# Frames ahead of weights at the start, the low-rank block alternating with its neighbour, and the recurrence's first loads on GpSimd's queue

## The chip, the cores and the metric

The kernel runs on one core of a Trainium2 chip. The metric is the device time of one execution in microseconds (us). Engines are named as in the profile: PE (TensorE matmul), PEld (its weight loads), DVE (VectorE), ACT (ScalarE), POOL (GpSimd), SP (SyncE, which here only issues DMAs). Each engine works through its own list of instructions in order, and waits at the head of that list for what the instruction there needs.

## The reference

One layer on 2048 frames of 1024 features, all in float32. A combined projection feeds a diagonal state space model (S5), a delta-rule recurrence (RWKV-7) and two gates; the branches are merged, projected, and followed by a feed-forward block with squared ReLU.

```
h = rmsnorm(x, norm1_g)
proj = h @ w_in                       # 1024 -> 512 + 1792 + 2048
u, p_rwkv, gate_a, gate_b = split(proj)
o_a = s5_branch(u)                    # 32 groups of 16 channels, scan over time, gelu, half-GLU
o_b = rwkv7_branch(p_rwkv)            # token shift, low-rank decay, state update per frame
merged = sigmoid(gate_a) * (o_a @ wb_a) + sigmoid(gate_b) * (o_b @ wb_b)
x = x + merged @ w_out
x = x + relu(rmsnorm(x) @ w1)**2 @ w2
out = rmsnorm(x)
# in rwkv7_branch: pm = p + (prev_frame(p) - p) * mu, cut into r, k, v, xg, xw, xa
# decay from tanh(xw) @ w2, a = sigmoid(a0 + xa @ a2), g = sigmoid(xg) @ g2
```

## The kernel before

Every large product is done as three matmuls on split operands: a weight w is cast to a rounded part (`wh`, on ACT or DVE) and a rest (`wl = w - wh`, on POOL), the same for the activations (`hh`, `hl`), and `mm3` (lines 121 to 123) issues wh x hl, wl x hh, wh x hh into the same PSUM tile. A window is 512 frames; there are NW = 4 of them. A block is one m (128 output features) of one window, 8 x 3 = 24 matmuls.

The program has four phases; the change is in the first two.

Phase A. `norm_window` loads four tiles of 128 frames (`xt`, line 452), sums their squares on ACT (line 145), makes the scale `rsa`, `rqa` on POOL (147, 149), scales on DVE (455), transposes on PE (462) and evicts into `hh` and `hl` (465, 466). `wu_load` loads the four blocks of the u projection (`wur`, 490), casts on DVE (491) and subtracts on POOL in two halves (493). At the start the two generators are woven step by step. Then come the u blocks, and then `dense()`: the projection for the recurrence, blocks m = 17, 16, 4 to 15, each for all four windows before the next. A block's PSUM tile (tag `mm`, four of them, shared with the low-rank products) is evicted by ACT (547) and DVE (548, 551, 555: the shift by one frame), into an `sg` tile (three of them), and stored to DRAM (`pm_d`). Block p17_w feeds `low_rank(w)`: a tanh, a split into `xh`, `xl`, and four pieces of six matmuls (`lr`, line 580) with two sigmoids each (`lo`, 583); a list `side` holds these pieces, and two are taken from it in each following block. `dense()` is woven with `s5_stream`, the S5 branch, eight groups q of channels: projections on PE (`px`, line 268), a scan on DVE (lines 380 to 403), products on PE and a gelu on ACT.

Phase B. `load(s)` reads the recurrence's inputs of 128 frames from DRAM (rm, km, vm, sgx, sig, aa). `elem(s)` prepares them (`kr`, then `sq`, `xh`, `xl`, the norm `n`, the scan `e`, `kf`, `km`, `BK`, `AG` and so on), `inv(s)` inverts small triangular systems, `chain(s)` runs the recurrence itself (`R` line 893, `U`, `S`, `y` line 915). They go in turns with `gates()`, the projection of the gates: `loadw` brings a weight block (`gwr`, then `gwh`, `gwl` 959) and 16 tiles of h (`gh`, 969) for a window; 64 blocks `gp` fill PE beside the recurrence.

Phases C and D (merge, output projection, feed-forward) follow and are not touched.

The order on each engine is not the program's order everywhere: a scheduler may move an instruction ahead of others on its engine where its operands allow it, unless `keep_in_program_order` (in the code: `pin`) holds it. In phase A and B the order of the generators' steps decides what stands where.

Of the kernel before, what the change touches and what calls it, by code (L numbers as in the profile page):

```python
# [21 lines left out]
NK = DM // 128  # L22
# [404 lines left out]
def phase_a(tc, nc, K, io, u_d, pm_d, h_d, z_d):  # L427
    with ExitStack() as st:
# [13 lines left out]
        with ExitStack() as s2:  # L442
# [68 lines left out]
        def load(m):  # L511
            wr = wp.tile([128, NK, 128], F32, tag="wr", name=f"wr{m}", bufs=1)
            nc.sync.dma_start(wr, io["win"][m])
            wh = wp.tile([128, NK, 128], F32R, tag="wh", name=f"wh{m}")
            wl = wp.tile([128, NK, 128], F32R, tag="wl", name=f"wl{m}")
            nc.scalar.copy(wh, wr)
            nc.gpsimd.tensor_tensor(wl, wr, wh, op=ALU.subtract)
            return wh, wl

        def dense():  # L520
            late = Late()
            nxt = first
            side = []
            for mi, m in enumerate(order):
                wh, wl = nxt
                if mi + 1 < len(order):
                    nxt = load(order[mi + 1])
                last = None
                if m % 3 == 0 and m < 16:
                    w = m // 3 - 2  # L530
                    o = 512 * (w % 2)
                    for j, H in enumerate((HH, HL)):
                        tc.keep_in_program_order(
                            nc.sync.dma_start(h_d[j, w], H[w // 2][:, :, o:o + 512].bitcast(F32)))
                i = m - 4
                for w in range(NW):
                    pp = psm.tile([128, 512], F32, tag="mm", name=f"p{m}_{w}")
                    o = 512 * (w % 2)
                    for k in range(NK):
                        mm3(nc, pp, wh[:, k], wl[:, k], HH[w // 2][:, k, o:o + 512], HL[w // 2][:, k, o:o + 512],  # L540
                            k == 0, k == NK - 1)
                        if k == 3:
                            yield
                        if side and k in (2, 6):
                            side.pop(0)()
                    sg = wp.tile([128, 512], F32, tag="sg", name=f"sg{m}_{w}", bufs=3)
                    nc.scalar.activation(sg, pp, ACTF.Copy, scale=om[:, i:i + 1])
                    nc.vector.scalar_tensor_tensor(sg[:, 1:512], pp[:, 0:511], mu[:, i:i + 1], sg[:, 1:512],
                                                   op0=ALU.mult, op1=ALU.add)
                    if w:  # L550
                        nc.vector.scalar_tensor_tensor(sg[:, 0:1], last, mu[:, i:i + 1], sg[:, 0:1],
                                                       op0=ALU.mult, op1=ALU.add)
                    if w < NW - 1:
                        last = wp.tile([128, 1], F32, tag="lc", name=f"lc{m}_{w}")
                        nc.vector.tensor_copy(last, pp[:, 511:512])
                    if m == 17:
                        side.extend(low_rank(w, sg))
                    else:
                        if m == 16:
                            nc.scalar.activation(sg, sg, ACTF.Sigmoid)  # L560
                        late.put(lambda i=i, w=w, sg=sg: nc.sync.dma_start(
                            pm_d[128 * i:128 * i + 128, 512 * w:512 * w + 512], sg))
                    yield
            late.flush()
# [35 lines left out]
def phase_b(tc, nc, K, io, pm_d, ob_d, h_d, gt_d, inv_d):  # L600
    V, A, P, T = nc.vector, nc.scalar, nc.gpsimd, nc.tensor
    NS = S // 128
    with ExitStack() as st:
# [46 lines left out]
        def load(s):  # L650
            d = D[s]
            for i, n in enumerate(("rm", "km", "vm")):
                d[n] = xp.tile([128, 4, 128], F32, tag=n, name=f"{n}{s}", bufs=3 if n == "vm" else 2)
                nc.sync.dma_start(d[n], pm_d[512 * i:512 * i + 512, 128 * s:128 * s + 128].rearrange(
                    "(h p) t -> p h t", p=128))
            d["sgx"] = xp.tile([128, 128], F32, tag="sgx", name=f"sgx{s}", bufs=4)
            nc.sync.dma_start(d["sgx"], pm_d[1536:1664, 128 * s:128 * s + 128])
            for i, n in enumerate(("sig", "aa")):
                d[n] = xp.tile([128, 4, 128], F32, tag=n, name=f"{n}{s}", bufs=2)
                nc.sync.dma_start(d[n], pm_d[1664 + 512 * i:2176 + 512 * i, 128 * s:128 * s + 128].rearrange(  # L660
# [8 lines left out]
        def elem(s):  # L669
            d = D[s]  # L670
            if s == 0:
                load(0)
# [205 lines left out]
        def chain(s):  # L878
# [3 lines left out]
            for c in range(2):  # L882
# [9 lines left out]
                for h in range(4):  # L892
                    T.matmul(rp[uc, 128 * h:128 * h + 128], AG[:, c, h, 0], S0[:, h, :], start=True, stop=True)
# [55 lines left out]
        def gates():  # L949
            late = Late()  # L950

            def loadw(m):
                pool = (gw, gt)[m % 2]
                wr = pool.tile([128, NK, 128], F32, tag="wr", name=f"gwr{m}")
                nc.sync.dma_start(wr, io["win"][18 + m % 16])
# [6 lines left out]
            nxt = loadw(0)  # L962
            for w in range(NW):
                hs = []
                for k in range(NK):
                    r = []
                    for i in range(2):
                        t = (gw if k < 5 else gt).tile([128, 512], F32R, tag=f"h{i}{k}", name=f"gh{w}_{i}{k}")
                        nc.sync.dma_start(t.bitcast(F32), h_d[i, w, :, k, :])
                        r.append(t)  # L970
                    hs.append(r)
                for _ in range(5):
# [18 lines left out]
        gg = Side(gates())  # L991
        next(gg)
# [864 lines left out]
```

## Time and profile before

| | |
|---|---|
| time, three runs | 3110.07, 3114.84 (median), 3119.49 us |
| profiled execution | 3106.43 us, its span 3104.7 us |
| mean granted PE clock | 0.97 |
| phase A ends (last p matmul) | about 548 us |
| PE busy in 500 to 540 | 37.56 of 40 us |
| PE busy in 600 to 610 | 4.86 of 10 us |

A row of the timeline has the start, the duration, the engine, the line, output and inputs by the program's names (the numbers of blocks and windows left out), their shapes, the count, and in brackets how long the engine had been idle before it and who ended that wait. SPq and POOLq are issues of DMAs. A clock below 1.00 means that the throttle granted PE less than its full speed.

### The profile page before, as it was taken

The page shows a single profiled execution, that of the slowest core. Times are in us where ns is not written, and L with a number is a line of the kernel's source. Part 1 is how long each engine was busy: PE and PEld are TensorE (multiplying, and loading weights), DVE is VectorE, ACT ScalarE, POOL GpSimd, SP SyncE. Part 2 cuts the span into 40 slices and gives each one's busy share as a digit, 9 for nine tenths or more (in the row PEclk, how much of TensorE's full clock was granted, in tenths as well). Part 3 has the DMA queues.
Part 4 walks back from the last instruction along what each step waited for, and adds up shares of the span by engine and source line. Part 5 has one row for each costly group of instructions (what it writes and reads, how often), then busy time and mean ns, then how long its engine had stood idle before and what let it go on. Part 6 is the DMA issues. An engine that isn't in the chain of part 4 may idle for free.

```text
span 3104.7 us, 45582 instructions
## 1 busy us (share of the span) xinstructions
PE 2928.6 (94%) x17024; PEld 2339.1 (75%) x17024; DVE 1942.6 (63%) x3307; ACT 1164.4 (38%) x1843; POOL 1333.7 (43%) x1117
## 2 busy tenths in 40 slices
PE   7989999589899999998999999999999999999998
PEld 5757777367677767777777878887788888888887
DVE  5348875367877777745333266656755566666667
ACT  4441211234343344324444455555333442222233
POOL 3100100645555455422433335555444655555564
PEclk9999999789899999999999999999999999999999
DMA  4344444534435334228656664333533386666664
GB/s 148 96 134 136 137 142 136 180 100 128 127 98 159 92 97 144 77 92 241 194 182 185 197 200 153 109 109 106 176 111 113 97 271 153 151 153 153 154 145 148
DMA packets 320157, 444.10 MB, mean 143 GB/s; under 512 B 112064, under 2 KB 173632, under 8 KB 319936
## 3 DMA queue, kind: packets, MB, share of 16 engines
q1 hardware_dynamic: 291776, 401.34, 40.6%
q0 software_dynamic: 11520, 35.66, 6.7%
q10 hardware_dynamic: 16640, 4.20, 0.5%
q8 instruction: 134, 2.20, 0.3%
q14 instruction: 87, 0.71, 0.1%
HBM read 302.55 MB, written 131.07 MB: 140 GB/s over the span
## 4 chain that ended last, share of the span: by engine, by line
PE 46%; DVE 5%; DMA 4%; issue 2%; POOL 2%; ACT 1%; SPq 0%; POOLq 0%; ACTq 0%; DVEq 0%
PE s L122 6%; PE s L123 6%; PE s L121 6%; PE f L121 5%; PE f L123 5%; PE f L122 5%; DMA wor<-in_wout_dram 1%; DMA g<-gt_d 1%; PE b L121 1%; PE b L122 1%; PE b L123 1%; PE o L121 1%; PE o L122 1%; PE o L123 1%; DVE bl L1318 1%
## 5 line engine op out<-in xcount | busy, mean ns | idle before, releaser
L121 PE MATMUL f<-bl,w1h 128*128 128x512 f32 x896 | 355.5, 397 | 8.9 <-ACT w1h L1345 8.9
L122 PE MATMUL f<-bh,w1l 128*128 128x512 f32 x896 | 351.8, 393 | 3.7 <-POOL w1l L1349 3.7
L123 PE MATMUL f<-bh,w1h 128*128 128x512 f32 x896 | 352.6, 394 | 0.0
L122 PE MATMUL s<-w2h,al 128*128 128x512 f32 x784 | 305.5, 390 | 1.0 <-POOL al L1563 1.0
L123 PE MATMUL s<-w2h,ah 128*128 128x512 f32 x784 | 305.4, 390 | 0.0
L121 PE MATMUL s<-w2l,ah 128*128 128x512 f32 x784 | 305.4, 390 | 0.0
L1349 POOL TENSOR_TENSOR w1l<-w1r,w1h 128x512 fp32r<-128x512 f32 x122 | 174.7, 1434 | 185.1 <-ACT w1h L1345 184.6
L121 PE MATMUL gp<-gh,gwh 128*128 128x512 f32 x512 | 228.8, 447 | 10.9 <-DMA gh<-h_d 10.8
L122 PE MATMUL gp<-gh,gwl 128*128 128x512 f32 x512 | 214.8, 420 | 6.4 <-POOL gwl L959 6.4
L1345 ACT CAST w1h<-w1r 128x512 fp32r<-128x512 f32 x224 | 137.7, 620 | 205.9 <-PE f L123 150.1
L1563 POOL TENSOR_TENSOR al<-ra,ah 128x1024 fp32r<-128x1024 f32 x64 | 167.4, 2617 | 108.0 <-ACT ah L1562 107.8
L123 PE MATMUL gp<-gh,gwh 128*128 128x512 f32 x512 | 211.1, 412 | 0.0
L1593 DVE TENSOR_TENSOR c<-c,s 128x512 f32<-128x512 f32 x224 | 149.9, 684 | 90.2 <-PE s L123 90.0
L121 PEld LDWEIGHTS f<-bl,w1h 128*128 128x128 f32 x896 | 169.8, 190 | 44.8 <-ACT w1h L1345 9.9
L122 PEld LDWEIGHTS f<-bh,w1l 128*128 128x128 f32 x896 | 169.6, 189 | 43.7 <-POOL w1l L1349 7.2
L123 PEld LDWEIGHTS f<-bh,w1h 128*128 128x128 f32 x896 | 169.3, 189 | 38.2
L959 POOL TENSOR_TENSOR gwl<-gwr,gwh 128x1024 fp32r<-128x1024 f32 x64 | 153.7, 2401 | 97.5 <-ACT gwh L958 81.8
L121 PE MATMUL p<-hl,wh 128*128 128x512 f32 x448 | 182.8, 408 | 3.6 <-ACT lo L583 3.6
L123 PE MATMUL p<-hh,wh 128*128 128x512 f32 x448 | 178.5, 399 | 0.0
L122 PE MATMUL p<-hh,wl 128*128 128x512 f32 x448 | 178.1, 398 | 0.0
L122 PEld LDWEIGHTS s<-w2h,al 128*128 128x128 f32 x784 | 147.3, 188 | 31.7 <-POOL al L1563 1.4
L123 PEld LDWEIGHTS s<-w2h,ah 128*128 128x128 f32 x784 | 147.3, 188 | 30.5
(382 smaller groups left out, 6995.1 us busy)
## 6 DMA issues: line engine op xcount, KB each, us to landing
gwr<-in_win_dram SPq DMA_DIRECT2D x64, 512.0 KB, 3.7
w1r<-in_w_dram SPq DMA_DIRECT2D x64, 512.0 KB, 3.4
r_d<-c SPq DMA_DIRECT2D x128, 256.0 KB, 2.0
ra<-r_d SPq DMA_DIRECT2D x64, 512.0 KB, 3.5
ch<-r_d POOLq DMA_DIRECT2D x42, 512.0 KB, 5.8
gh<-h_d SPq DMA_DIRECT2D x64, 256.0 KB, 5.0
gt_d<-gs SPq DMA_DIRECT2D x64, 256.0 KB, 2.8
g<-gt_d SPq DMA_DIRECT2D x64, 256.0 KB, 3.4
```

Of the source, the lines that this page charges most:

```text
L121: nc.tensor.matmul(ps, wh, xl, start=start, stop=False)
L122: nc.tensor.matmul(ps, wl, xh, start=False, stop=False)
L123: nc.tensor.matmul(ps, wh, xh, start=False, stop=stop)
L959: P.tensor_tensor(wl, wr, wh, op=ALU.subtract)
L1318: V.tensor_tensor(l[k], o, h[k], op=ALU.subtract)
L1345: cast = A.copy(h, o)
L1349: (P if n % 2 or edge else V).tensor_tensor(l, o, h, op=ALU.subtract)
L1563: P.tensor_tensor(l, raw[n], h, op=ALU.subtract)
L1593: V.tensor_tensor(d, d, bank, op=ALU.add if i in (4, 5, 6) else ALU.subtract)
```

## The change

First, the four steps of `norm_window(0)` that load and scale x0 to x3 run before the weave with `wu_load` begins.

Second, `dense()` runs over groups (m, w): for each window first m = 17, then m = 16, and then blocks 4 to 15 as before. The last column of a window, which the next window of the same block needs, is kept for each m (`lasts`). A step that does nothing is put ahead of each window's four low-rank pieces. The weights of block 4 are loaded at group 5 and split at group 7.

Third, in phase B `load(0)`, the first gate weights `gwr0` and the ten tiles of `gh` with k below 5 of window 0 are issued by POOL instead of SP, `load(0)` before the turns begin and ahead of `gwr0`'s split, which now stands behind the gh loads.

Fourth, the R products are pinned to the program's order.

```diff
-                weave(norm_window(0, x8), wu_load(x8))
+                n0 = norm_window(0, x8)
+                for _ in range(4):
+                    next(n0)
+                weave(n0, wu_load(x8))
...
-        def load(m):
+        def raw(m):
             wr = wp.tile([128, NK, 128], F32, tag="wr", name=f"wr{m}", bufs=1)
             nc.sync.dma_start(wr, io["win"][m])
+            return wr
+
+        def load(m, wr=None):
+            wr = wr or raw(m)
...
-            nxt = first
-            side = []
-            for mi, m in enumerate(order):
-                wh, wl = nxt
-                if mi + 1 < len(order):
-                    nxt = load(order[mi + 1])
+            W = {order[0]: first, order[1]: load(order[1])}
+            side, lasts = [], {}
+            groups = [(m, w) for w in range(NW) for m in order[:2]] + [(m, w) for m in order[2:] for w in range(NW)]
+            for gi, (m, w) in enumerate(groups):
+                wh, wl = W[m]
+                if gi == 2 * NW - 3:
+                    ahead = raw(order[2])
+                elif gi == 2 * NW - 1:
+                    W[order[2]] = load(order[2], ahead)
+                elif w == 0 and m not in order[:2] and m != order[-1]:
+                    W[m + 1] = load(m + 1)
...
+                if m == 17:
+                    side.append(lambda: None)
+                    side.extend(low_rank(w, sg))
...
-        def load(s):
+        def load(s, q=nc.sync):
...
-            if s == 0:
-                load(0)
...
-                    T.matmul(rp[uc, 128 * h:128 * h + 128], AG[:, c, h, 0], S0[:, h, :], start=True, stop=True)
+                    pin(T.matmul)(rp[uc, 128 * h:128 * h + 128], AG[:, c, h, 0], S0[:, h, :], start=True, stop=True)
...
-            nxt = loadw(0)
+            wr0 = raww(0, nc.gpsimd)
+            yield
...
-                        nc.sync.dma_start(t.bitcast(F32), h_d[i, w, :, k, :])
+                        (nc.sync if w or k >= 5 else nc.gpsimd).dma_start(t.bitcast(F32), h_d[i, w, :, k, :])
...
+                if w == 0:
+                    nxt = loadw(0, wr0)
...
         gg = Side(gates())
+        next(gg)
+        load(0, nc.gpsimd)
         next(gg)
```

On POOL at the very start, before (`rsa`, `rqa` are the scale of a tile of frames, `wul` the rest of a block of u weights):

```order
L147 TENSOR_SCALAR rsa_113<-ssa_111 128x1
L493 TENSOR_TENSOR wul<-wur_120,wuh 128x512
L149 TENSOR_TENSOR rqa_115<-rsa_113,mhalf 128x1
L147 TENSOR_SCALAR rsa_130<-ssa_128 128x1
L149 TENSOR_TENSOR rqa_132<-rsa_130,mhalf 128x1
L493 TENSOR_TENSOR wul<-wur_135,wuh 128x512 x2
L147 TENSOR_SCALAR rsa_145<-ssa_143 128x1
L149 TENSOR_TENSOR rqa_147<-rsa_145,mhalf 128x1
L493 TENSOR_TENSOR wul<-wur_150,wuh 128x512 x2
L147 TENSOR_SCALAR rsa_160<-ssa_158 128x1
L149 TENSOR_TENSOR rqa_162<-rsa_160,mhalf 128x1
L493 TENSOR_TENSOR wul<-wur_165,wuh 128x512 x2
```

and now:

```order
L147 TENSOR_SCALAR rsa_113<-ssa_111 128x1
L149 TENSOR_TENSOR rqa_115<-rsa_113,mhalf 128x1
L147 TENSOR_SCALAR rsa_123<-ssa_121 128x1
L149 TENSOR_TENSOR rqa_125<-rsa_123,mhalf 128x1
L147 TENSOR_SCALAR rsa_133<-ssa_131 128x1
L149 TENSOR_TENSOR rqa_135<-rsa_133,mhalf 128x1
L147 TENSOR_SCALAR rsa_143<-ssa_141 128x1
L149 TENSOR_TENSOR rqa_145<-rsa_143,mhalf 128x1
L493 TENSOR_TENSOR wul<-wur_164,wuh 128x512 x2
L493 TENSOR_TENSOR wul<-wur_183,wuh 128x512 x2
L493 TENSOR_TENSOR wul<-wur_202,wuh 128x512 x2
```

The four scales stand ahead of all subtractions instead of between them. SP's loads go the same way: x0, x1, x2, x3 and then the four blocks of weights, where a block of weights followed each tile of frames before.

On DVE at the end of the first S5 scan, before (the L39x to L403 rows are the scan's last steps, `sg17_3` the eviction of block 17 of the last window, `sg16_0` that of block 16 of the first):

```order
L398 TENSOR_TENSOR f20_1_1731<-NI_607,X_1264 128x434
L397 TENSOR_TENSOR f10_1_1730<-A8_606,X_1264 128x434
L401 TENSOR_TENSOR f10_1_1730<-f10_1_1730,f20_1_1731 128x434
L403 TENSOR_TENSOR X_1264<-X_1264,f10_1_1730 128x2x31x7
L548 SCALAR_TENSOR_TENSOR sg17_3_1565<-p17_3_1504,vec_73,sg17_3_1565 128x511
L551 SCALAR_TENSOR_TENSOR sg17_3_1565<-lc17_2_1489,vec_73,sg17_3_1565 128x1
L572 TENSOR_TENSOR xl2_1492<-sg17_2_1485,xh2_1491 128x512
```

and now:

```order
L398 TENSOR_TENSOR f20_1_1698<-NI_607,X_1264 128x434
L397 TENSOR_TENSOR f10_1_1697<-A8_606,X_1264 128x434
L401 TENSOR_TENSOR f10_1_1697<-f10_1_1697,f20_1_1698 128x434
L558 SCALAR_TENSOR_TENSOR sg17_2_1609<-p17_2_1548,vec_73,sg17_2_1609 128x511
L561 SCALAR_TENSOR_TENSOR sg17_2_1609<-lc17_1_1470,vec_73,sg17_2_1609 128x1
L565 COPY lc17_2_1613<-p17_2_1548 128x1
L403 TENSOR_TENSOR X_1264<-X_1264,f10_1_1697 128x2x31x7
L583 TENSOR_TENSOR xl2_1616<-sg17_2_1609,xh2_1615 128x512
```

The eviction of window 2 of block 17 stands where that of window 3 stood; those of p17_1 and p16_1 stand inside the scan.

On POOL at the beginning of phase B, before (behind the last subtraction of phase A and five memsets):

```order
L791 MEMSET Y_5341 128x512
L959 TENSOR_TENSOR gwl_4604<-gwr_4601,gwh_4603 128x1024
L793 COPY YC_4898<-cstb 64x256
L793 COPY YC_5344<-cstb 64x256
L722 TENSOR_TENSOR xl_4743<-sq_4666,xh_4742 128x512
L695 COPY cmid<-e_4681 128x4x2
```

and now (rows of the inputs rm, km, sgx, sig, aa stand ahead of the first; nine more gh loads, `gwl` and `cmid` follow the last):

```order
L731 TENSOR_TENSOR xl_4743<-sq_4666,xh_4742 128x512
L963 DMA gwr_4601<-in_win_dram 128x1024
L983 DMA gh_00_4615<-h_d 128x512
L647 MEMSET geps 128x1
L651 MEMSET eend 128x132
L654 MEMSET SB_4597 128x512
L654 MEMSET SB_4598 128x512
L665 DMA vm_4607<-pm_d 128x4x128
L983 DMA gh_10_4617<-h_d 128x512
```

The step `xl` of the recurrence's preparation goes ahead of the first gates' loads, and twelve loads go between it and the split of the first gate weights. On PE at the place where the first products of the recurrence stand, before:

```order
L893 MATMUL R_5214<-SB_4597,AG_4774 64x128 x4
L915 MATMUL y_5210<-AG_4774,SB_4597 64x64
L121 MATMUL gp_4730<-gh_10_4609,gwh_4670 128x512
L745 MATMUL bo_4801<-rm_4639,cstb 128x512
L122 MATMUL gp_4730<-gh_00_4607,gwl_4671 128x512
```

and now:

```order
L121 MATMUL gp_4730<-gh_10_4617,gwh_4670 128x512
L924 MATMUL y_5210<-AG_4774,SB_4597 64x64
L754 MATMUL bo_4801<-rm_4603,cstb 128x512
L122 MATMUL gp_4730<-gh_00_4615,gwl_4671 128x512
L123 MATMUL gp_4730<-gh_00_4615,gwh_4670 128x512
```

R has gone from there (it stands behind the inversion's last products now), and y has stayed.

More of the change, by code (lines that the diff above doesn't have):

```diff
@@ new lines, in dense @@
+            for gi, (m, w) in enumerate(groups):
[6 more added lines that the diff above has]
+                    W[m + 1] = load(m + 1)
+                if m % 3 == 0 and m < 16 and w == 0:
+                    v = m // 3 - 2
+                    o = 512 * (v % 2)
@@ L532, in dense @@
                     for j, H in enumerate((HH, HL)):
                         tc.keep_in_program_order(
-                            nc.sync.dma_start(h_d[j, w], H[w // 2][:, :, o:o + 512].bitcast(F32)))
+                            nc.sync.dma_start(h_d[j, v], H[v // 2][:, :, o:o + 512].bitcast(F32)))
                 i = m - 4
[L536 to L548, printed above, removed]
-                                                   op0=ALU.mult, op1=ALU.add)
[L550 to L563, printed above, removed]
@@ new lines, in dense @@
+                pp = psm.tile([128, 512], F32, tag="mm", name=f"p{m}_{w}")
+                o = 512 * (w % 2)
+                for k in range(NK):
+                    mm3(nc, pp, wh[:, k], wl[:, k], HH[w // 2][:, k, o:o + 512], HL[w // 2][:, k, o:o + 512],
+                        k == 0, k == NK - 1)
+                    if k == 3:
+                        yield
+                    if side and k in (2, 6):
+                        side.pop(0)()
+                sg = wp.tile([128, 512], F32, tag="sg", name=f"sg{m}_{w}", bufs=3)
@@ new lines, in dense @@
+                nc.scalar.activation(sg, pp, ACTF.Copy, scale=om[:, i:i + 1])
+                nc.vector.scalar_tensor_tensor(sg[:, 1:512], pp[:, 0:511], mu[:, i:i + 1], sg[:, 1:512],
+                                               op0=ALU.mult, op1=ALU.add)
+                if w:
+                    nc.vector.scalar_tensor_tensor(sg[:, 0:1], lasts[m], mu[:, i:i + 1], sg[:, 0:1],
+                                                   op0=ALU.mult, op1=ALU.add)
+                if w < NW - 1:
+                    lasts[m] = wp.tile([128, 1], F32, tag=f"lc{m % 2}", name=f"lc{m}_{w}")
+                    nc.vector.tensor_copy(lasts[m], pp[:, 511:512])
@@ L564, in dense @@
+                if m == 17:
+                    side.append(lambda: None)
+                    side.extend(low_rank(w, sg))
+                else:
+                    if m == 16:
+                        nc.scalar.activation(sg, sg, ACTF.Sigmoid)
+                    late.put(lambda i=i, w=w, sg=sg: nc.sync.dma_start(
+                        pm_d[128 * i:128 * i + 128, 512 * w:512 * w + 512], sg))
+                yield
             late.flush()
@@ L653, in load @@
                 d[n] = xp.tile([128, 4, 128], F32, tag=n, name=f"{n}{s}", bufs=3 if n == "vm" else 2)
[L654 removed]
+                q.dma_start(d[n], pm_d[512 * i:512 * i + 512, 128 * s:128 * s + 128].rearrange(
                     "(h p) t -> p h t", p=128))
             d["sgx"] = xp.tile([128, 128], F32, tag="sgx", name=f"sgx{s}", bufs=4)
[L657 removed]
+            q.dma_start(d["sgx"], pm_d[1536:1664, 128 * s:128 * s + 128])
             for i, n in enumerate(("sig", "aa")):
                 d[n] = xp.tile([128, 4, 128], F32, tag=n, name=f"{n}{s}", bufs=2)
[L660 removed]
+                q.dma_start(d[n], pm_d[1664 + 512 * i:2176 + 512 * i, 128 * s:128 * s + 128].rearrange(
                     "(h p) t -> p h t", p=128))
@@ L950, in gates, with raww, loadw @@
             late = Late()
-            def loadw(m):
+            def raww(m, q=nc.sync):
+                wr = (gw, gt)[m % 2].tile([128, NK, 128], F32, tag="wr", name=f"gwr{m}")
+                q.dma_start(wr, io["win"][18 + m % 16])
+                return wr
+            def loadw(m, wr=None):
                 pool = (gw, gt)[m % 2]
-                wr = pool.tile([128, NK, 128], F32, tag="wr", name=f"gwr{m}")
-                nc.sync.dma_start(wr, io["win"][18 + m % 16])
+                wr = wr or raww(m)
                 wh = pool.tile([128, NK, 128], F32R, tag="wh", name=f"gwh{m}")
@@ L960, in loadw @@
                 return wh, wl
-            nxt = loadw(0)
+            wr0 = raww(0, nc.gpsimd)
+            yield
             for w in range(NW):
```

4 lines of the change are left out of this document (removed).

## The prediction

> **What bounds the kernel now.** The list of busy time by engine comes first, then the windows by stage, then the waits inside the stages that are not full.
>
> ```profile
> PE 2928.6 (94%) x17024; PEld 2339.1 (75%) x17024; DVE 1942.6 (63%) x3307; ACT 1164.4 (38%) x1843; POOL 1333.7 (43%) x1117
> ```
>
> TensorE (PE) is busy for 94% of the span, and the change takes no matmul away. So all that can be won is the other 6%, some 176 us, and only the part of it that lies where the change works. The windows (width, then busy time and count of PE, PEld, DVE, ACT, POOL, then the granted clock, the DMA share and GB/s) show those places:
>
> ```profile
> 0.00:25.00 25.00, 4.47 (x16) 2.86 (x16) 5.99 (x11) 6.98 (x11) 12.43 (x21) 1.00 0.89 337
> 100.00:150.00 50.00, 50.00 (x228) 38.77 (x227) 17.61 (x43) 18.50 (x23) 10.44 (x15) 1.00 0.38 106
> 170.00:180.00 10.00, 5.19 (x21) 2.80 (x19) 9.55 (x20) 1.99 (x3) 1.12 (x1) 0.97 0.34 102
> 180.00:190.00 10.00, 5.75 (x15) 3.72 (x15) 2.93 (x7) 3.20 (x5) 0.00 (x0) 0.51 0.33 99
> 550.00:560.00 10.00, 2.86 (x7) 1.87 (x8) 0.00 (x0) 0.30 (x1) 2.81 (x3) 0.58 1.02 351
> 570.00:580.00 10.00, 1.22 (x2) 0.50 (x2) 6.04 (x6) 4.16 (x7) 9.54 (x15) 0.60 1.03 298
> 580.00:590.00 10.00, 1.73 (x10) 1.57 (x10) 7.03 (x10) 2.51 (x4) 9.82 (x10) 0.50 0.09 27
> ```
>
> PE idles for 20.5 us at the start, 9.1 us at 170 to 190, and 24.2 us in the three windows of 550 to 590. Between them it is full (50.00 of 50), so time won ahead of a full stretch is carried through it. Each part of the change has one of these places.
>
> **The start.** The timeline from 5 to 30 us:
>
> ```profile
> 5.28 1.06 ACT L145 ACTIVATE jk<-xt 128x1024 f32<-128x1024 f32 x1 [3.27 <-DMA xt<-in_x_dram]
> 14.09 1.06 ACT L145 ACTIVATE jk<-xt 128x1024 f32<-128x1024 f32 x1 [1.42 <-DMA xt<-in_x_dram]
> 17.72 0.75 DVE L455 TENSOR_SCALAR xt<-xt,rqa 128x1024 f32<-128x1024 f32 x1 [3.50 <-POOL rqa L149]
> 19.16 2.48 POOL L493 TENSOR_TENSOR wul<-wur,wuh 128x512 fp32r<-128x512 f32 x2 [1.47 <-DVE wuh L491]
> 22.58 0.75 DVE L455 TENSOR_SCALAR xt<-xt,rqa 128x1024 f32<-128x1024 f32 x1 [3.50 <-POOL rqa L149]
> 23.39 1.12 PE L462 MATMUL pt<-csta,xt 128*128 128x128 f32 x4 [3.74 <-DVE xt L455]
> 26.20 0.78 PE L121 MATMUL u<-hl,wuh 128*128 128x512 f32 x1
> 28.11 0.19 ACT L145 ACTIVATION_READ_ACCUMULATOR jk<-xt 128x1 f32 x1
> 29.24 0.75 DVE L455 TENSOR_SCALAR xt<-xt,rqa 128x1024 f32<-128x1024 f32 x1 [1.18 <-POOL rqa L149]
> ```
>
> The square sums of x0 and x3 (the first two rows) begin as those tiles land, six transfers of 512 KB apart, three of frames and three of weights: 8.81 us, or 1.47 us each. The frames alone would be three apart, so x3's would begin at 5.28 + 3 * 1.47 = 9.7 us and be done with its 1.06 and 0.19 at 10.9. Now x3's scale waits on POOL behind a 2.48 us subtraction of weights and DVE twice waits 3.50 us for a scale. With the scales first, the distance of a later tile holds: its sum is read out at 28.30, DVE's product begins at 29.24, 0.94 later. So x3 is scaled from 11.9 to 12.6, and its transposes begin 0.06 us later (23.39 behind 23.33), at 12.7 in place of 23.39: 10.7 us earlier. The weights do not take this back: the first is the fifth transfer, 5.28 + 4 * 1.47 = 11.2 us, its cast on DVE stands behind x3's scaling (as long as that, 0.75, by my estimate: to 13.4), and the first half of its subtraction on POOL (2.48 for two) ends at 14.6; the first product of u would stand at 26.20 - 10.7 = 15.5. The three others land 1.47 us apart, while a block of u takes 24 matmuls of 0.22 us (50.00 us over 228). I take **-10 us**. If one 3.50 us wait stays, -7; -10.7 is the other end. What follows in the stage is full PE, which carries the shift.
>
> **The low-rank block.** Its waits (engine, line, waited for; total, times, longest) and its timeline:
>
> ```profile
> PE lr L580 <- DVE sg L548: 6.9, 1, 6.9
> 155.01 0.37 DVE L380 TENSOR_TENSOR m<-X,A 128x128 f32<-128x128 f32 x1
> 163.63 0.72 DVE L548 SCALAR_TENSOR_TENSOR sg<-p,vec,sg 128x511 f32<-128x511 f32 x1
> 181.31 0.74 DVE L548 SCALAR_TENSOR_TENSOR sg<-p,vec,sg 128x511 f32<-128x511 f32 x1
> 174.69 0.50 PE L580 MATMUL lr<-xl,lrh 64*128 64x512 f32 x1
> 182.27 0.63 ACT L570 ACTIVATE sg<-sg 64x512 f32<-64x512 f32 x1 [7.67 <-DVE sg L551]
> 185.90 0.79 PE L121 MATMUL p<-hl,wh 128*128 128x512 f32 x1 [2.15 <-ACT lo L583]
> ```
>
> DVE runs the S5 scan of one group of channels from 155.01 to 181.31 with two things slipped in. p17_3's eviction stands behind it in DVE's order; PE needs that PSUM tile and waits from 175.19 to 182.10, ACT for its tanh too. Alternation does not shorten the scan. It only puts other blocks under it: after the change p17_1 and p16_1 are evicted inside and p17_2 behind the second f product (the rows in the section on the change). Counted from the scan's input products to the matmul that must wait for the eviction behind the scan, PE has 69 matmuls of p in place of 48 and about as many of lr (29, before 31). So PE comes there 21 * 0.22 = 4.6 us later, less 0.3, or at 179.5 in the old times. The scan carries one eviction more (about 1 us), so the tile is free at 183. The wait shrinks from 6.9 to about 3.5, it does not go: **-3.5 us**. The 2.15 us wait for ACT's lo behind it is as likely as before. Ends: all 9.1 us of the two windows won, or 3 us lost, if the lr pieces that start one slot later meet ACT's sigmoids in a worse order.
>
> On the clock: after the 6.9 us wait the row of 180 to 190 shows 0.51. The Trainium skill ("TensorE: Matmul & The Clock Gate", Part 1) says that the clock drops after an idle window of about 3.4 us; by it a wait of 3.5 us stands just on that edge, and no row here decides it. I leave the clock as it is in the sum; were the clock full there, the 15 matmuls in 5.75 us of that window would take 15 * 0.22 = 3.3, and the sum would be 2.4 us better, 3090.
>
> **The transition to the recurrence.** Rows of SP, ACT, POOL, DVE and PE around it, then the two classes of DMA that POOL issues elsewhere (durations min, median, max in ns; the landing row is the first class's) and the window of the second:
>
> ```profile
> 536.88 0.69 ACT L547 ACTIVATE sg<-p,om 128x512 f32<-128x512 f32 x1 [4.91 <-PE p L123]
> 548.06 0.98 POOL L791 MEMSET Y<- 128x512 f32 x2 [22.45 <-PE p L123]
> 549.74 2.34 POOL L959 TENSOR_TENSOR gwl<-gwr,gwh 128x1024 fp32r<-128x1024 f32 x1 [0.69 <-ACT gwh L958]
> 550.55 10.88 SPq L969 DMA_DIRECT2D gh<-h_d x16
> 552.10 0.73 POOL L793 COPY YC<-cstb 64x256 f32<-64x256 f32 x2
> 568.38 0.69 DVE L681 TENSOR_TENSOR kr<-km,vec 128x512 f32<-128x512 f32 x1 [18.75 <-DMA km<-pm_d]
> 570.47 2.23 POOL L722 TENSOR_TENSOR xl<-sq,xh 128x512 fp32r<-128x512 f32 x1 [17.63 <-ACT xh L721]
> 572.64 0.19 POOL L695 COPY cmid<-e 128x8 f32<-128x8 f32 x1
> 587.17 2.05 POOL L736 TENSOR_TENSOR AG<-AR,gam 128x512 f32<-128x512 f32 x2
> 588.27 1.33 PE L893 MATMUL R<-SB,AG 128*64 128x128 f32 x5 [14.30 <-POOL AG L736]
> L1500 POOL DMA_DIRECT2D ch<-r_d x28: 864/887/1457, 2475.0 to 2963.8; - x28
> L1650 POOL DMA_DIRECT2D u<-s x8: 869/3068/3487, 2969.5 to 2980.0; - x8
> DMA to landing us min/median/max: 5.2/5.5/11.0
> 2969.00:2982.00 13.00, 13.00 (x59) 10.77 (x58) 8.94 (x11) 4.11 (x4) 12.92 (x11) 1.00 1.09 241
> ```
>
> Before, the recurrence's inputs wait on SP behind 16 loads of gates, so kr starts at 568.38; from there POOL's chain, xl, cmid and so on to AG (572.64 to 589.22, 16.6 us without a gap), ends last, and PE stands on AG for 14.30 us.
>
> After, POOL issues the inputs. The first can go when p15_1 is done (536.88; an estimate, since its tile lies where that stage's tiles lay); rm and km at 0.89 us each go by 538.7, and km lands 5.5 us after its issue at 537.8, at 543.3. From kr to xl it takes 570.47 - 568.38 = 2.1: xl runs from 545.4 to 547.6. Then 12 issues (gwr0, vm0, ten of gh) at 0.89 make 10.7, the two memsets of SB among them 1.0 (as those of Y), gwl0 2.3, and the chain 16.6 plus the fills of Y and YC, which lay in idle time and now lie in it, 0.98 + 0.73. AG ends at 547.6 + 10.7 + 1.0 + 2.3 + 18.3 = 579.9, in place of 589.2: **-9 us**. The first block of gates needs gwl0 (561.6) and is done before AG, as it was.
>
> What the pin removes is less than it says: the R products leave their place, but the first y product, which is not pinned and reads the same AG, stands there in their stead, ahead of gp1. PE still waits for AG.
>
> The unknown is POOL's issue. The two rows give 0.89 and 3.07 us. The long ones were issued amid DVE work (8.94 us of that window's 13), and in 550 to 560 DVE shows 0.00, so I take 0.89. At SP's rate (10.88 / 16 = 0.68) the gain is 12; at 3.07, five issues delay xl to 554.5, twelve take 36.8, and AG ends at 613, 24 us later than now.
>
> The Trainium skill ("SBUF — State Buffer", the trap that DVE blocks DMA) speaks against this edit: GpSimd writes its descriptors through a port that some DVE instructions lock, and it gives 620 ns for a DMA alone and 3100 ns beside them. The rows' 0.87 and 3.07 fit that; the idle DVE here would put it at the short end for the first loads, and only a DVE that has begun its chain could stretch the last ones; with 3100 ns for each the sum would be that of the slower rival below.
>
> **Sum.** -10 - 3.5 - 9 = -22.5. The profiled run took 3106.43 us (its span 3104.7), so 3084 for its like; it lies 8.4 under the median of 3114.84, which gives **3092**. The stages behind keep their program and move along.
>
> **The rivals.** A measurement of this kernel can tell about 0.3%, 9.3 us, from no change.
>
> *The waits only change their names* (0.18). The start gains its 7 to 10, but the low-rank wait stays whole under p17_2, and y stands on AG as long as R did, because POOL's twelve issues come before gwl0. This needs issues of about 1.6 us: 547.6 + 12 * 1.6 + 21.6 = 588.4. For it: the chain is POOL's either way. Against it: the inputs land 20 us earlier. Time: 3106.4 - 7 + 8.4 = 3108.
>
> *POOL's queue becomes the bound* (0.07), the one that is slower. With p us for an issue AG ends at 560.7 + 17p once p is over 1.7, and the transition loses what that is over 589.2. Against the 13.5 won elsewhere the kernel is slower from 2.5 us an issue, and by over 0.3% from 3.0; at 3.07 the sum is -13.5 + 24 = +10, 3125. For it is the row of 3068; against it the idle DVE.
>
> *The early frames do not pay* (0.10). If S5's preparation or later frames stall PE between 30 and 150 us, where it is full now, the 10 us are lost there: -12.5, 3102. It needs PE waits where the windows show none.
>
> *More than forecast* (0.10): the wait at 175 gone and the chain shorter, -10.7 - 9.1 - 12 = -32, 3083.
>
> **Chances.** The forecast, 3085 to 3100, has 0.55. The range of 8 in 10 runs from 3078 to 3111, the ends of the terms (-32 to -7) with some 4 us for the median's own spread (3110.07 to 3119.49). Faster by over 0.3% is 0.75, from the forecast, the larger gain and most of the lost start; within 0.3% is 0.18, slower 0.07.
>
> **What would show it.** The start: PE's first product of u near 16 us and no 3.50 us wait of DVE. Low rank: one PE wait of 3 to 4 us for a DVE eviction or its copy near 165 to 175. Transition: ten gh issues on POOL of under 1 us each, xl near 535 and AG ending near 566 (13.5 us earlier clock), and a y product, not R, waiting for it. The forecast is wrong if POOL's issues show 2 us or more, if gp0 waits for gwl0 beyond 550 on that clock, or if PE shows waits between 20 and 140.

## The result and the profile after

The changed kernel takes 3087.94 us (median of four, 3077.49 to 3096.0) against 3115.95 us before on the same chip: a ratio of 0.9915 with a 95% interval of [0.989, 0.994], some 26 us. Its profiled run took 3077.49 us, the fastest of the four, with a span of 3075.7 us in place of 3104.7, so the trace shows more than the median gained. The list of busy time and the windows by stage (columns as before):

```profile
PE 2910.2 (95%) x17024; PEld 2325.8 (76%) x17024; DVE 1950.6 (63%) x3307; ACT 1165.5 (38%) x1845; POOL 1353.8 (44%) x1134
0.00:25.00 25.00, 13.71 (x56) 10.62 (x57) 11.71 (x18) 13.45 (x22) 12.06 (x22) 1.00 0.90 345
25.00:50.00 25.00, 23.42 (x117) 18.94 (x116) 20.70 (x94) 18.75 (x31) 13.05 (x22) 1.00 0.23 71
150.00:160.00 10.00, 7.87 (x32) 5.12 (x31) 9.45 (x28) 3.90 (x6) 0.00 (x0) 1.00 0.55 156
170.00:190.00 20.00, 20.00 (x98) 14.49 (x99) 8.54 (x21) 10.31 (x16) 3.46 (x5) 1.00 0.51 147
200.00:250.00 50.00, 39.59 (x179) 30.02 (x176) 28.27 (x75) 17.90 (x26) 3.44 (x5) 0.90 0.45 136
540.00:550.00 10.00, 3.20 (x6) 1.84 (x7) 4.28 (x3) 2.53 (x3) 6.42 (x11) 0.50 1.01 353
550.00:560.00 10.00, 6.83 (x21) 4.16 (x20) 5.98 (x6) 1.89 (x4) 9.46 (x16) 0.84 1.06 363
560.00:570.00 10.00, 3.66 (x6) 1.47 (x7) 4.37 (x9) 3.70 (x5) 9.85 (x11) 0.50 0.41 127
```

PE works 13.71 us of the first 25 in place of 4.47, the hole of 170 to 190 is gone (20.00 of 20), but one of 10.41 us has opened in 200 to 250. In the transition PE still works less than 7 us in each of the three windows of 10, two of them at half clock. Three timelines show why. The start:

```profile
12.90 0.75 DVE L455 TENSOR_SCALAR xt<-xt,rqa 128x1024 f32<-128x1024 f32 x1 [0.71 <-POOL rqa L149]
16.52 0.78 PE L121 MATMUL u<-hl,wuh 128*128 128x512 f32 x1
26.82 2.99 POOL L493 TENSOR_TENSOR wul<-wur,wuh 128x512 fp32r<-128x512 f32 x2
30.74 0.75 DVE L455 TENSOR_SCALAR xt<-xt,rqa 128x1024 f32<-128x1024 f32 x1 [2.08 <-POOL rqa L149]
31.55 0.33 PE L462 MATMUL pt<-csta,xt 128*128 128x128 f32 x1 [0.44 <-DVE xt L455]
33.02 0.77 PE L462 MATMUL pt<-csta,xt 128*128 128x128 f32 x5 [1.14 <-DVE xt L455]
121.70 0.40 PE L121 MATMUL p<-hl,wh 128*128 128x512 f32 x1
129.20 0.40 PE L121 MATMUL p<-hl,wh 128*128 128x512 f32 x1
```

The last two rows are the first p matmul of the kernel after and of the kernel before. x3 is scaled at 12.90 (forecast 11.9) and the first product of u stands at 16.52 in place of 26.20. Two short waits at 31.55 and 33.02 are new: tiles of the second window wait for scales that stand on POOL behind the last block's subtraction (26.82). At the first p matmul 7.5 of the 9.7 us are left; the two waits are 1.6 of the 2.2 lost.

The low-rank block (waits, then the timeline of DVE and PE with one window, from 160 to 162, among its rows; the last row is the same px of the kernel before):

```profile
PE lr L591 <- DVE lc L565: 10.4, 1, 10.4
PE lr L591 <- DVE xl L583: 2.0, 1, 2.0
227.19 0.74 DVE L558 SCALAR_TENSOR_TENSOR sg<-p,vec,sg 128x511 f32<-128x511 f32 x1
227.98 0.15 DVE L565 COPY lc<-p 128x1 f32<-128x1 f32 x1
160.00:162.00 2.00, 2.00 (x7) 1.25 (x8) 1.93 (x7) 0.69 (x1) 0.00 (x0) 0.50 0.36 135
228.28 0.79 PE L591 MATMUL lr<-xl,lrh 64*128 64x512 f32 x2 [10.41 <-DVE lc L565]
258.78 1.95 PE L268 MATMUL px<-uT,E 128*64 128x256 f32 x16
269.43 1.95 PE L268 MATMUL px<-uT,E 128*64 128x256 f32 x16
```

Under the first scan no more than 2.0 us are waited, for `xl` and not for an eviction; behind this wait the granted clock stands at 0.50 from 160 to 162, and in the second trace of this kernel too. The pieces of the last window have slid past the second scan's start, and there one of them waits 10.41 us for an eviction that stands at its end. At the third group's px (258.78 against 269.43) the lead is 10.6 us, 3.1 more than at the first p.

The transition, with POOL's issues of gh as one group of the lines view (busy, mean ns, idle before and its releasers) in the last row:

```profile
524.61 0.69 ACT L557 ACTIVATE sg<-p,om 128x512 f32<-128x512 f32 x1 [4.91 <-PE p L123]
524.84 1.01 POOL L665 DMA_DIRECT2D rm<-pm_d  x1 [25.44 <-PE p L123]
531.65 0.69 DVE L690 TENSOR_TENSOR kr<-km,vec 128x512 f32<-128x512 f32 x1 [5.37 <-DMA km<-pm_d]
533.74 1.29 POOL L731 TENSOR_TENSOR xl<-sq,xh 128x512 fp32r<-128x512 f32 x1 [5.08 <-DMA km<-pm_d]
534.99 0.57 POOL L963 DMA_DIRECT2D gwr<-in_win_dram  x1
546.35 2.36 POOL L972 TENSOR_TENSOR gwl<-gwr,gwh 128x1024 fp32r<-128x1024 f32 x1
565.20 2.05 POOL L745 TENSOR_TENSOR AG<-AR,gam 128x512 f32<-128x512 f32 x2
566.30 0.47 PE L924 MATMUL y<-AG,SB 128*64 128x64 f32 x2 [4.29 <-POOL AG L745]
L983 POOL DMA_DIRECT2D gh<-h_d x10 | 5.4, 541 | 3.6 <-DMA gwr<-in_win_dram 1.6 <-DMA gh<-h_d 1.4 <-DMA vm<-pm_d 0.5
```

The first load leaves POOL as p15_1 ends, and AG starts 565.20 - 524.61 = 40.6 us behind it, where it took 587.17 - 536.88 = 50.3 before.

### The profile page after: what moved, and what is told of

It reads as the page before. It is cut to its first block, busy times and chain, and to the rows that moved or that the text cites. A ratio compares the mean times of both kernels' runs of the same rounds, so it can differ in the third digit from the quotient of the medians.

```text
span 3075.7 us, 45604 instructions
## 1 busy us (share of the span) xinstructions
PE 2910.2 (95%) x17024; PEld 2325.8 (76%) x17024; DVE 1950.6 (63%) x3307; ACT 1165.5 (38%) x1845; POOL 1353.8 (44%) x1134
## 3 DMA queue, kind: packets, MB, share of 16 engines
q1 hardware_dynamic: 287408, 396.82, 40.6%
## 4 chain that ended last, share of the span: by engine, by line
PE 53%; DVE 12%; DMA 7%; issue 3%; POOL 3%; SPq 1%; ACT 1%; DVEq 0%; POOLq 0%; ACTq 0%
PE f L121 6%; PE f L123 6%; PE f L122 6%; PE s L122 6%; PE s L123 6%; PE s L121 6%; DVE YC L816 2%; DVE yt L814 2%; DMA wor<-in_wout_dram 2%; PE gp L121 2%; DMA g<-gt_d 2%; PE gp L123 2%; PE gp L122 2%; PE b L121 1%; PE b L123 1%
## 5 line engine op out<-in xcount | busy, mean ns | idle before, releaser
L121 PEld LDWEIGHTS f<-bl,w1h 128*128 128x128 f32 x896 | 169.7, 189 | 45.4 <-ACT w1h L1363 10.4
L121 PEld LDWEIGHTS s<-w2l,ah 128*128 128x128 f32 x784 | 147.2, 188 | 30.5
```

The costliest lines, as they stand in the source:

```text
L121: nc.tensor.matmul(ps, wh, xl, start=start, stop=False)
```

## The experiments

Places that every trace has, as us of the span for the kernel before and as the difference to it for the others ("again" is a second trace of the same kernel):

| place | before | before again | after | after again | start alone | low rank alone | POOL alone |
|---|---|---|---|---|---|---|---|
| first u product | 26.2 | -0.4 | -9.7 | -10.5 | -10.4 | -0.3 | -0.7 |
| first p | 129.2 | +0.4 | -7.5 | -8.3 | -8.2 | +0.5 | -0.9 |
| third px | 269.4 | +0.9 | -10.6 | -11.3 | -6.5 | -3.7 | -0.5 |
| first AG starts | 587.2 | +0.6 | -22.0 | -22.7 | -5.8 | -5.1 | -11.6 |
| 257th gates matmul | 711.7 | -0.1 | -29.5 | -29.7 | -5.9 | -11.8 | -14.6 |
| last gates matmul | 1399.4 | -5.1 | -30.5 | -20.4 | -2.2 | -9.0 | -20.8 |
| end of span | 3104.7 | 0.0 | -28.9 | -18.5 | +5.2 | -2.3 | -18.3 |

The expectations below call the 257th gates matmul the third window of the gates; it stands in the eleventh block.

**The start alone.**

```diff
-                weave(norm_window(0, x8), wu_load(x8))
+                n0 = norm_window(0, x8)
+                for _ in range(4):
+                    next(n0)
+                weave(n0, wu_load(x8))
```

> The kernel before with the first part alone. My theory: the part is independent of the others. The first u product moves from 26.2 to 16.5 us, the fourth eviction of u from 55.2 to about 48.3, and from the first p matmul to the last the trace runs 7.5 us earlier than before; the whole kernel is 7 to 8 us faster (about 3108). Rival: part of the 9.7 us is lost again by the S5 scan or the low-rank wait, whose 6.9 us wait on DVE would grow: then the last p matmul is less than 5 us earlier.

Ratio 0.9993, [0.9976, 1.001]: from 7 us faster to 3 us slower. The trace has the lead as expected up to AG (-8.2, -6.5, -5.8), and loses it behind, where nothing was changed: -2.2 at the last gates matmul, +5.2 at the end. The first half of the expectation holds, that this is 7 to 8 us of the whole time is not shown. The low-rank wait did cost it 1.7 us (-8.2 to -6.5), as the rival had it, but less than the rival's bound.

**The low-rank block alone.** The kernel before with the new `dense()`:

```diff
-            for mi, m in enumerate(order):
+            groups = [(m, w) for w in range(NW) for m in order[:2]] + [(m, w) for m in order[2:] for w in range(NW)]
+            for gi, (m, w) in enumerate(groups):
...
+                    side.append(lambda: None)
                     side.extend(low_rank(w, sg))
```

> The kernel before with the second part alone. Theory from the trace after: the 6.9 us wait under the first S5 scan is gone and a wait of about 10 us stands under the second scan, where the low-rank pieces now reach; from px1 to px2 the two together leave a gain of about 3 us at px2 (269.4 before, about 266 now). Rival, my prediction on record: one wait of about 3.5 us under the first scan and nothing under the second, with the same gain. A third: alternation gains nothing without the earlier start (px2 at 269).

Ratio 0.9987, [0.997, 1.0003]. Its timeline has the wait, and at the third px a lead of 3.7 us:

```profile
235.00 0.80 PE L588 MATMUL lr<-xl,lrh 64*128 64x512 f32 x2 [10.09 <-DVE lc L562]
```

So the wait under the second scan belongs to the alternation and not to its meeting with the earlier start. My forecast of one wait of 3.5 us under the first scan is refuted.

**The loads on POOL and the pin alone.** The kernel before with the new phase B:

```diff
-            nxt = loadw(0)
+            wr0 = raww(0, nc.gpsimd)
+            yield
...
+        load(0, nc.gpsimd)
```

> The kernel before with the third and fourth part alone (loads on POOL, R pinned). Theory: the distance from the end of p15_1 to the end of AG shrinks from 52.3 us to about 42.6, as in the trace after, and the whole kernel is about 10 us faster. Rival: some 7 us more come behind AG (the trace after gained 7.4 us between AG and the third window of the gates), and it is 17 us faster.

Ratio 0.9962, [0.9949, 0.9976], 7 to 16 us: the one part that shows by itself. From its two rows, p15_1's end to AG's end takes 575.61 + 2.41 - 536.40 = 41.6 us.

```profile
536.40 0.69 ACT L547 ACTIVATE sg<-p,om 128x512 f32<-128x512 f32 x1 [4.91 <-PE p L123]
575.61 2.41 POOL L734 TENSOR_TENSOR AG<-AR,gam 128x512 f32<-128x512 f32 x2 [1.29 <-DVE AR L730]
```

The three ratios alone add up to 0.58% (2.2 + 4.0 + 11.8 = 18 us), the whole change to 0.85% and, below, 0.66%: within the intervals they add.

**The same order on SP's queue.**

```diff
-            wr0 = raww(0, nc.gpsimd)
+            wr0 = raww(0)
...
-        load(0, nc.gpsimd)
+        load(0)
```

and all gh on `nc.sync`.

> The kernel after with load(0), gwr0 and all gh issued by SP again, in the order of the program, so load(0) ahead of gh and no DMA on POOL. Theory that the order matters and not the queue: km still lands early, POOL has no issues and no waits for landings ahead of gwl0, and the distance from the end of p15_1 to the end of AG is 40 to 45 us, time equal to the kernel after within 5 us. Rival that the queue matters: SP holds the loads back behind its stores and the constants, kr starts 8 us or more later than in the trace after, the distance is near 50, and the kernel is 7 to 10 us slower than after.

Ratio 0.9962, [0.994, 0.9984], against 0.9915 and 0.9934 for the change: slower than both, though against the second the intervals overlap. Neither theory has it whole. AG comes even sooner, 563.42 + 2.42 - 527.84 = 38.0 us behind p15_1, though kr starts 20.4 us behind it in place of 7.0. But then the gates stop, waiting for their second weight block, whose load stands on SP behind all of gh and load(1):

```profile
527.84 0.69 ACT L557 ACTIVATE sg<-p,om 128x512 f32<-128x512 f32 x1 [4.91 <-PE p L123]
563.42 2.42 POOL L745 TENSOR_TENSOR AG<-AR,gam 128x512 f32<-128x512 f32 x2 [1.29 <-DVE AR L741]
582.53 0.80 PE L121 MATMUL gp<-gh,gwh 128*128 128x512 f32 x1 [10.19 <-ACT gwh L971]
```

So against this run the change has AG later and the second block of gates sooner (561.2 us). Which of POOL's loads that comes from, this run can't tell, since it moves them all; the run with only gh on SP, further down, takes them apart.

**The change again.** No edit.

> The changed kernel again, beside the others on this chip, for a second trace. Theory: the trace shows again about -7.5 us at the first p matmul, -10.5 at px2, and AG about 40.6 us behind the end of p15_1; what came behind AG in the first trace (-22 at AG, -29.5 at the third gates' window) is not the change's and may be anything between 0 and 8 us here. Rival: the 7 us behind AG come again, as a part of the change.

Ratio 0.9934, [0.9913, 0.9955], about 20 us. The table has its trace: up to the 257th gates matmul it repeats the first within 1 us, the 7 us behind AG too. Then it loses 9 us up to the last gates matmul, and ends at -18.5. So the 7 us come again, as the rival said, and 10 us of difference between two traces of one kernel lie behind them. They go with the granted clock: its mean is 0.975 in the first trace and 0.970 in the second, and over the 31 runs of the kernel before that were taken beside the first experiments (3094.55 to 3118.68 us) the time rises by 2.1 us for each thousandth that this mean is lower, with a correlation of -0.81. By that, five thousandths are an estimated 10.5 us.

**Without the empty step.**

```diff
-                    side.append(lambda: None)
```

> The kernel after without the step that does nothing ahead of each window's low-rank pieces. Theory: the wait of 10.4 us stands under the second S5 scan because the pieces of the last window reach into it; without the empty step the last piece stands right behind px1, and that wait is gone; px2 comes 5 to 10 us earlier than in the trace after (258.8), unless waits of up to 7 us come back under the first scan. Rival: the empty step is what keeps the pieces clear of the first scan, and px2 comes later than 259.

Ratio 0.9939, [0.9916, 0.9962]. The wait under the second scan is gone, and waits under the first are back, the exception that the theory had made:

```profile
PE lr L590 <- DVE xl L582: 8.2, 3, 5.6
256.39 1.95 PE L268 MATMUL px<-uT,E 128*64 128x256 f32 x16
```

The third px is 1.8 to 2.4 us sooner than in the two traces after, of which nothing is left at the last p matmul (-13.0 there, -12.3 and -12.9 in those). The step moves the wait from one scan to the next and is worth nothing that the time shows.

**Without the pin.**

```diff
-                    pin(T.matmul)(rp[uc, 128 * h:128 * h + 128], AG[:, c, h, 0], S0[:, h, :], start=True, stop=True)
+                    T.matmul(rp[uc, 128 * h:128 * h + 128], AG[:, c, h, 0], S0[:, h, :], start=True, stop=True)
```

> The kernel after without the pin on R. Theory: no difference beyond 1 us at AG, at the second block of gates and at the third window, since the y product stands at the same place and waits for the same AG; R is back beside it. Rival: R's return costs PE's wait on AG again, as the 14.3 us of before, and the second block of gates starts 5 us or more later than in the trace after.

Ratio 0.9926, [0.9906, 0.9946], no different from the change. AG and the second block of gates are the same within 1.2 us, R waits for AG where y waited: the theory holds there, but not at the 257th gates matmul, 687.7 against 682.3. The rows are two U products, the first and a later one at the same place of the program, and windows, of this run and then of the kernel after:

```profile
635.99 1.96 PE L908 MATMUL U<-Rs,Y 64*64 64x64 f32 x16
685.58 1.11 PE L908 MATMUL U<-Rs,Y 64*64 64x64 f32 x16 [1.09 <-DVE Rs L904]
636.00:642.00 6.00, 6.00 (x78) 5.66 (x78) 2.19 (x5) 1.62 (x2) 2.28 (x1) 0.55 0.12 44
668.00:676.00 8.00, 6.06 (x69) 5.02 (x70) 5.23 (x7) 1.73 (x3) 6.25 (x5) 0.57 0.73 210
```

```profile
635.75 1.14 PE L908 MATMUL U<-Rs,Y 64*64 64x64 f32 x16
680.20 1.11 PE L908 MATMUL U<-Rs,Y 64*64 64x64 f32 x16 [1.17 <-DVE Rs L904]
636.00:680.00 44.00, 39.98 (x444) 31.44 (x441) 34.68 (x63) 15.88 (x26) 24.46 (x23) 1.00 0.39 115
```

From one U to the other it takes 49.6 us without the pin and 44.4 with it, where the clock stands at 1.00 throughout. Here it is low at both ends. What the clock lacks there, 0.45 of 6 us and 0.43 of 8 us, is 6.1 us, about the difference. Over all traces the stretch takes 42.1 to 45.8 us with the pin (nine of nine), 49.6 to 50.2 in four without it (before twice, start alone, this run) and 45.2 in one without (low rank alone). So it goes by where the low clock falls, and the pin goes with that, but for the one trace; whether it brings it about stays open, and the ratio does not show it.

**All gh on SP, inputs and first weights on POOL.**

```diff
-                        (nc.sync if w or k >= 5 else nc.gpsimd).dma_start(t.bitcast(F32), h_d[i, w, :, k, :])
+                        nc.sync.dma_start(t.bitcast(F32), h_d[i, w, :, k, :])
```

> The kernel after with all gh loads on SP; load(0) and gwr0 stay on POOL. Theory: POOL's chain to AG no longer has ten issues and their 3.6 us of waits for landings in it, and AG starts 36 to 39 us behind the end of p15_1 in place of 40.6; the gates' second block does not start later, since SP issues gh as fast as POOL. Rival: SP's own queue (16 issues of 0.65 us and load(1) ahead of gwr1) delays the second gate weights, the second block of gates starts as late as in the run with everything on SP, and the kernel is no faster than after.

Ratio 0.9924, [0.990, 0.9948]. POOL's chain to AG was shortened by more than I thought: without the ten issues AG starts 554.95 - 527.04 = 27.9 us behind p15_1, not 36 to 39. The wait went over to the gates, as the rival said, though their second block is not as late as with everything on SP (47.5 us behind p15_1 against 54.7), and took the 12 us back:

```profile
554.95 2.42 POOL L745 TENSOR_TENSOR AG<-AR,gam 128x512 f32<-128x512 f32 x2 [0.69 <-DVE AR L741]
574.51 0.80 PE L121 MATMUL gp<-gh,gwh 128*128 128x512 f32 x1 [10.18 <-ACT gwh L971]
```

From the run with everything on SP this one differs only in that the inputs and the first gate weights are on POOL. That brings AG 7.7 us nearer to p15_1 (27.9 in place of 35.6), the third block of gates 8.6 (56.8 in place of 65.4) and the 257th gates matmul 8.7 (157.0 in place of 165.7), with a ratio of 0.9924 in place of 0.9962 (the intervals just overlap). So, by these two traces, these are the loads that pay on POOL. The ten gh loads beside them only move the wait between AG and the gates: in the change the 257th gates matmul stands 157.7 us behind p15_1, and the ratios can't be told apart.

**The second gate weights from POOL, behind the first steps of the recurrence; and the same without the empty step.**

```diff
             wr0 = raww(0, nc.gpsimd)
             yield
+            wr1 = raww(1, nc.gpsimd)
...
-                        nxt = loadw(j + 1)
+                        nxt = loadw(j + 1, None if j else wr1)
```

> The run with gh on SP, and the load of the second gate weights gwr1 issued by POOL, behind the first recurrence steps and ahead of AG. Theory: with gh on SP, AG was 12 us nearer to p15_1's end but the second block of gates waited 10.2 us for gwh1, whose load stood behind gh and load(1) on SP; with gwr1 from POOL that wait is under 2 us, the second block of gates starts with the end of the first, near 564, and the third block near 575 in place of 583.8. The time is then 3 to 8 us below the kernel after. Rival: the gates' loads are bound by what the DMA engines move (over 300 GB/s from 540 to 560 in the trace after), gwr1 takes from gh what it gains, and the third block of gates starts within 2 us of the kernel after's 576.5.

> The same, and without the empty step ahead of the low-rank pieces. Theory: px2 is 1.5 to 2 us earlier than in the run before this one, and the whole at best that much faster, which a measurement cannot tell. Rival: the two together lose.

Ratios 0.9929, [0.9907, 0.9951], and 0.9916, [0.9895, 0.9936]: neither can be told from the change. The second block of gates does start at once (563.7), and then the third waits for its weights, 9.24 us, with the DMA engines at a share of 1.06 from 540 to 560:

```profile
579.67 0.79 PE L121 MATMUL gp<-gh,gwh 128*128 128x512 f32 x1 [9.24 <-ACT gwh L971]
540.00:560.00 20.00, 8.18 (x16) 4.68 (x17) 11.68 (x15) 5.55 (x8) 16.66 (x22) 0.56 1.06 345
```

It starts at 579.7, 3.2 us behind the kernel after's 576.5, but p15_1 ends 2.5 us later in this trace; counted from there it is 0.7 us, within the rival's 2. Without the empty step the third px came 2.7 us earlier than in the run before it (255.6), more than the 1.5 to 2 expected, and the time does not show it. Whatever is loaded first, some next block's weights are late, and the DMA engines' share is 1.01 and 1.06 in the same two windows of the change. That what they move is the bound is argued only: no run here moved fewer bytes. No version here is shown to beat the change.

**DVE kept busy beside POOL's issues.** 32 copies behind kr, extra work:

```diff
+            if s == 0:
+                for _ in range(32):
+                    pin(V.tensor_copy)(fl(ep.tile([128, 4, 128], F32, tag="e3", name="junk")), fl(kr))
```

> The kernel after with 32 copies of 128 x 512 float32 from SBUF to SBUF on DVE behind the first kr, extra work that only keeps DVE busy while POOL issues gwr0, vm0 and gh. Theory of the lock: the issues on POOL that fall beside these copies take 1.5 to 3.5 us in place of 0.55, the last gh issue moves 10 us or more behind xl, and gwl0 with it. Rival: POOL's issues stay at 0.5 to 0.8 us each (DVE's work is not what made the 3.07 us ones of the merge stage long), and only DVE's own chain is late by the copies' 12 to 16 us.

```profile
539.67 3.70 POOL L986 DMA_DIRECT2D gh<-h_d  x7
539.97 3.66 DVE L678 COPY junk<-kr 128x512 f32<-128x512 f32 x7
545.38 2.96 DVE L678 COPY junk<-kr 128x512 f32<-128x512 f32 x1
545.69 2.35 POOL L975 TENSOR_TENSOR gwl<-gwr,gwh 128x1024 fp32r<-128x1024 f32 x1
549.04 1.80 DVE L678 COPY junk<-kr 128x512 f32<-128x512 f32 x4
```

Seven issues beside the copies take 3.70 us, 0.53 each: the theory of the lock falls, for plain loads beside such copies. The ten gh loads land no later either (median 5.8 us behind their issue, 7.7 in the kernel after), and gwl0 is not late: it starts 18.7 us behind p15_1 here and 21.7 in the kernel after. It is DVE that gives way, a little beside the issues and wholly beside POOL's own work: a copy takes 1.80 / 4 = 0.45 us by itself, 3.66 / 7 = 0.52 beside the issues, and the one beside gwl takes 2.96, ending 0.3 us behind it. Its single run took 3094.99 us.

**The kernel before again.** No edit.

> The kernel before once more, for a second trace of it. Theory: up to the end of the p matmuls and to AG the two traces agree within 1 us, and behind AG they differ by several us, as the clock is granted differently; a stretch of about 24 us at half clock near 644 may or may not be there. Rival: it is there again and of the same length, and the kernel before always has it.

Up to AG it repeats within 1 us, at the last gates matmul it is 5.1 us ahead, at the end level (3106.46 us). The half clock behind AG is there again, in pieces. The window of 24 us in the first trace of before and in the second:

```profile
644.00:668.00 24.00, 22.69 (x236) 18.28 (x237) 14.06 (x20) 6.13 (x12) 15.90 (x19) 0.51 0.31 92
```

```profile
644.00:668.00 24.00, 20.20 (x244) 16.36 (x244) 14.04 (x20) 6.14 (x12) 15.76 (x19) 0.69 0.33 99
```

The theory holds for the lengths, the rival in that the low clock is no accident of one trace.

## Why the prediction was right

It forecast -22.5 us and 3092, a ratio of 0.9927; the runs gave 3087.94, and ratios of 0.9915 and 0.9934 that mean 26 and 20 us. The ratio is the fairer test: beside other batches the kernel before itself took 3106 to 3110 us at the median. The size and the three places were right, and two of the three terms came out by errors that cancel, which is luck. Step by step:

- **The start, -10.** Right in mechanism: x3 scaled at 12.9, first product 9.7 to 10.8 us sooner than in the first trace of before in all traces that have it. Too large by 1.3 to 2.5 at the first p matmul (-7.5 to -8.7). The step that failed is "what follows in the stage is full PE, which carries the shift": it holds behind 34 us, but before that the second window's scales wait on POOL behind the last subtraction, 0.44 + 1.14 us of PE; the other 0.6 us of the loss have no wait in the trace. It is the rival of the early frames, in small, and waits between 20 and 140 were a sign of being wrong by the forecast's own list. Alone, the start shows in the trace to AG and not in the time.
- **The low-rank block, -3.5.** The size came out, 3.1 and 3.0 in the two traces and 4.2 alone (from +0.5 to -3.7), and the mechanism did not. I counted matmuls to the wait under the first scan and found 3.5 us left for an eviction; 2.0 are left there, and for `xl`. I did not follow the last pieces past the second px, where the empty step had pushed them: 10.4 us. The hole of 9.1 us was filled, another was opened, and that the difference is the forecast is luck.
- **The transition, -9.** The size came out, AG 9.7 us nearer to p15_1, by two errors that cancel: POOL's issue of gh takes 0.54 us and not 0.89, with the others 4 us less in all, and four issues waited 3.6 us for landings, which I had not seen. I had taken 0.89 from the wrong kind of transfer: all that POOL issues in the kernel before are accumulating ones (`accum_op=ALU.add`, lines 1495, 1500 and 1650), and those moved here are plain loads. y waits for AG as foreseen, but for 4.3 us. And AG is not what the time goes by alone: with gh on SP it came 12.7 us sooner still, counted from p15_1, and the time stayed, since the gates' weights then came late; I had no term for these.
- **POOL's queue as the bound.** The condition of this rival, issues of 2.5 us and more, did not come up, and DVE's copies did not bring it about. The Trainium skill ("SBUF — State Buffer", the trap that DVE blocks DMA, and the section "A bandwidth-pool intuition that's wrong") gives about 3100 ns in place of 620 for a DMA from GpSimd beside a DVE copy; here seven issues beside float32 copies within SBUF took 0.53 us each, and their loads landed no later, so for these the measurement decides against the page. What made the u<-s issues long was not tried. They are accumulating transfers and stand amid POOL's own subtractions, so DVE is not the only candidate.
- **"The stages behind keep their program and move along."** Not quite: both traces after gain 7 us more between AG and the 257th gates matmul. I cost the pin at nothing. 5 of the 7 are a stretch free of half clock that goes with the pin in all traces but one; whether the pin brings it about is open. It does not carry safely: the second trace gave 9 us back by the end of phase B, and the ratio without the pin is the same.
- **The clock.** I left it as it was, since a wait of 3.5 us seemed to stand just on an edge; a wait of 2.0 us was already followed by 0.50 (160 to 162). It is the largest thing that I did not foresee: the 10.5 us between the two traces after go with it, and so 29 us of a trace and 20 to 26 us of ratios can be the same change.

## What to carry to other kernels

When work that a slow engine's long job delays is dealt out anew, follow the last of its pieces to the end: a wait that leaves one place may stand at the next such job. When a queue is moved, look at what waited behind it on the old queue as well as at what it brings sooner: here AG came soonest with only the inputs and the first weights on POOL, and the time did not follow, since the next weights then came late. When an issue is priced from rows elsewhere, see that they are the same kind of transfer: an accumulating one is no price for a plain load. Places compared in two traces of each kernel tell how far a gain of 0.2% repeats, and from where on it is no more than the spread.

## What the runs showed of the hardware

- An issue of a plain load on POOL took 0.54 us for 256 KB (ten gh in 5.4) and 0.57 us for 512 KB (gwr0). The accumulating 512 KB transfers of the kernel before (line 1500) took 0.89.
- Four of POOL's issues stood still until an earlier DMA of the same queue had landed (1.62, 0.84, 0.53 and 0.58 us). By the order of names each waited for the eighth before it: gh with k = 3 for gwr0, and so on. The trace's records show why: POOL's loads use eight semaphores, 111 to 118, in turn, and each of the four waits for the one that it is to use again. So this is the program's limit; a limit of the chip is not shown.
- Beside seven POOL issues of plain loads a DVE copy of 128 x 512 float32 within SBUF took 0.52 us in place of 0.45; beside a POOL subtraction of 2.35 us one took 2.96.
- A wait of 2.0 us on PE was followed by a granted clock of 0.50 (160 to 162, in both traces after).
- The granted clock stood at 0.51 for 24 us (644 to 668 in the first trace of before) while PE was busy for 22.69 of them, without a gap from 645.31 on, and at 0.69 in the same window of the second: the same program, and another clock.
